# A gated attention, pooling and SSD trunk on one core: the relative position table's products moved between the turns of the first two x blocks, the branch norm done with a matrix of ones, both softmax statistics turned at once

## The chip, the core and the metric

The kernel runs on one core of one Trainium2 chip. The time is device microseconds of that core for one whole execution. Lower is better. Verdicts compare medians of several runs of the two kernels on the same chip.

## The reference, cut to what matters

One layer on x of 512 tokens by 1024 features, in float32. Three branches read the same normed input, are gated and summed, then projected; a convolutional feed-forward block follows.

```python
u = rmsnorm(x, ln1_g[i])
proj = u @ w_in[i]
q, k, v, pool_in, z, xbc, dt_raw, gate_pre = jnp.split(proj, split_idx, axis=-1)
y_a = dilated_attention_mixer(q, k, v, rel_bias) @ w_a[i]
y_b = pool_mixer(pool_in, pool_w[i], pool_scale[i]) @ w_b[i]
y_c = ssd_mixer(z, xbc, dt_raw, ...) @ w_c[i]
gates = jax.nn.sigmoid(gate_pre + b_gate[i]).reshape(b, s, N_BRANCH, D_MODEL)
merged = gates[:, :, 0] * y_a + gates[:, :, 1] * y_b + gates[:, :, 2] * y_c
x = x + merged @ w_o[i]
x = x + conv_ffn(rmsnorm(x, ln2_g[i]), ...)
out = rmsnorm(x, final_g)

# attention: three groups of six heads, dilations 1, 4, 16, each a causal band
bias = bias_table[bucket]                      # the relative position table
m = max(scores); p = exp(scores - m); l = sum(p)
o = (p @ v) / l; lse = m + log(l)
alpha = softmax(stack(lses), axis=groups)      # the groups are weighed by lse
o = sum(alpha * o)

# the SSD branch's norm, over each of two groups of 512 features
y = y.reshape(b, s, SSD_INNER) * jax.nn.silu(z)
yg = y.reshape(b, s, SSD_GROUPS, SSD_INNER // SSD_GROUPS)
yg = yg * lax.rsqrt(jnp.mean(yg * yg, axis=-1, keepdims=True) + NORM_EPS)
y = yg.reshape(b, s, SSD_INNER) * norm_w
```

## The kernel before, in words

Every large product is made of fp32r matmuls in three parts: each factor is split into a high part (a cast to fp32r on ACT) and a low part (the difference, on DVE), and high*high, high*low and low*high are summed in PSUM (`mm3`, L234). Tokens or features are laid on the 128 partitions, 512 on the free side. Weights come in blocks called jobs of 1 MB or less. For job n the kernel issues, before its products, the low part of job n+1 (L215, `wl`), the cast of job n+2 in two halves (L195, `wh`) and the fetch of job n+3 (L183, `raw`, two buffers). The fetch waits until the low part that read the buffer before is done.

The order on PE, ACT, DVE and POOL is the order in which the program issues instructions (`ORDERED`). Each of these engines runs its own list in that order and waits only for data and buffers. SP is left out of that list: a planner places its DMAs, by the times that it works out, and they need not stand in the order of the program.

Small work is threaded between the large products by coroutines. `step()` is called after each 128-feature chunk of a product (24 matmuls of 512 columns for eight k-blocks). It takes one coroutine from `waiting` into `running` and advances all of those that run by one `yield`. Within a step there are phases (0, ROWS, WHOLE, REST); `yield WHOLE` holds the coroutine until that phase of the same step, where the transposes and small products of PE stand. Thus a coroutine's instructions of one step stand on each engine's list behind those of the coroutines that joined `running` earlier, and before the next job's low part.

PSUM has eight banks: four tagged "mm" for the large products, four tagged "sm" for the small ones. SBUF tiles of 128x512 float32 come from one pool of 54 slots through `T(name)`.

The places that the change touches:

- The opening (`load_x`, `warm_up`, `turn_scale`, the loop over two blocks). x is loaded as eight tiles of 128 tokens by 512 features (`xin`). For the first two token blocks the row norm's factor is put on the diagonal of a matrix (`diag`, from the identity `eye`), and PE turns the block with it (`uT`, L1574): one product both transposes and scales. Twelve warm-up products run before that. g1 (the norm's weight) is turned between the two blocks (L1590) and copied by DVE (L1591). `turned` writes uh (ACT) and ul (DVE); `begin` (L1557) makes the first two chunks of the pool branch's projection.
- `bias_rows`: loads the bias table and a one-hot table (`hot`, 33 rows by 896) and returns `rows`, in which PE multiplies the two (`psr`, L532, four products in float32), DVE copies the result (`rv`), and SP stores it in DRAM (`rdram`) and reads it back in shifted rows as six tiles `b`. `rows` ran as a coroutine behind the pool branch's first products, inside the first group's v product (`pb`, a flipped product with 400 columns).
- `attend(g)`: attention of one group. The row maxima (`nm`) and sums (`ls`) of six heads by four blocks are turned at the end by `stats`, eight transposes into two banks (`pst`, L786), and copied by DVE (`nmT`, `lsT`). `combine` makes the groups' weights of them: on DVE up to the reciprocal (L811), POOL's product (L815), stores to DRAM (`wd`), and 18 loads `wb`, by which POOL multiplies the outputs `o` (L824).
- `ssd_prep`: per-head constants, among them `dgc`, which holds the skip weight and the norm's weight.
- `gated(gi, j, z)` and `y_norm(gi)`: y*z and its square for each of four chunks of a half (`sq`, ACT); the squares are summed by POOL and, the last, by DVE (L1094). Then `y_norm` sums over the features on PE (`pss`, L1104, four float32 products with one column), `rstd_of` makes the reciprocal square root on ACT and DVE, DVE puts it on four diagonals (`dg`, L1108), and PE spreads it over all partitions by a product with ones (`prb`, L1115). DVE multiplies y by it (L1118), and y is split into `yth` and `ytl`.

Around the branch norm the order is given by `MIX = "ZZ0zz1ggggaa"`: two z jobs of the first half, y_norm(0) queued, two z jobs of the second half, y_norm(1) queued, four jobs of the third gate, then the attention's output product.

Of the kernel before, what the change touches and what calls it, by code (L numbers as in the profile page):

```python
# [10 lines left out]
F32 = mybir.dt.float32  # L11
# [72 lines left out]
def trunk(ctx: ExitStack, tc, out, x, rel_bias, ln1_g, w_in, b_gate, w_a, pool_w, pool_scale, w_b,  # L84
# [37 lines left out]
    ones = cpool.tile([P, P], F32, name="ones")  # L122
# [388 lines left out]
    def bias_rows():  # L511
# [4 lines left out]
        sp.dma_start(relb[:BUCKETS, :18], rel_bias)  # L516
        sp.dma_start(hot[0][:BUCKETS + 1, :S], c_hot[:, :S])
        sp.dma_start(hot[1][:BUCKETS + 1, :R_ALL - S], c_hot[:, S:])
# [5 lines left out]
        def rows():  # L524
            rv = [T(f"rv{i}") for i in range(2)]
            rd = dram.tile([HEADS, R_ALL], F32, name="rdram")
            ps_r = [SM("psr0"), SM("psr1")]
            for g, (off, n) in enumerate(zip(R_OFF, R_LEN)):
                lo = off
                while lo < off + n:  # L530
# [3 lines left out]
                    lo += m  # L534
            for i in range(2):
                m = (S, R_ALL - S)[i]
                dve.tensor_copy(rv[i][:HEADS, :m], ps_r[i][:HEADS, :m])
                sp.dma_start(rd[:, i * S:i * S + m], rv[i][:HEADS, :m])
# [8 lines left out]
            return  # L547
            yield
# [23 lines left out]
    dtr = cpool.tile([P, 4, SH], F32, name="dtr")  # L572
    V, QK, OT, NM, LS = {}, {}, {}, {}, {}
# [133 lines left out]
    def attend(g):  # L707
        nm = cpool.tile([P, 4, HEADS], F32, name=f"nm{g}")
        ls = cpool.tile([P, 4, HEADS], F32, name=f"ls{g}")
# [71 lines left out]
        def stats():  # L781
            yield WHOLE
            for src, store, nme in ((nm, NM, "nmT"), (ls, LS, "lsT")):
                ps = SM("pst")
                for n in range(4):
                    pe.transpose(ps[:HEADS, n * P:(n + 1) * P], src[:, n, :], eye)  # L786
                t = T(nme)
                dve.tensor_copy(blocked(t[:HEADS], g), grouped(ps[:HEADS], g))
                store[g] = t
# [114 lines left out]
    def ssd_prep():  # L904
# [39 lines left out]
        pe.matmul(ps[:, n16:2 * n16], ones, a, start=True, stop=True)  # L944
        for i, r in enumerate((dr, gr)):
            pe.transpose(ps[:, 2 * n16 + 8 * i:2 * n16 + 8 * i + 8], r[:8, :P], eye[:8, :8])
        dve.tensor_copy(dgc, ps[:, 2 * n16:2 * n16 + 16])
        acs, tot, dec = (f(nme) for nme in ("acs", "tot", "dec"))
# [35 lines left out]
    def ssd_item(c, gi):  # L984
        cs = slice(c * P, (c + 1) * P)
        dtv, acs, dec, tot, ad, ed = (cst[n] for n in ("dtv", "acs", "dec", "tot", "ad", "ed"))
# [109 lines left out]
    def y_norm(gi):  # L1096
        while len(SQ[gi]) < 4:
            yield
        yield
        yield  # L1100
        yield WHOLE
        ps = SM("pss")
        for tb in range(4):
            pe.matmul(ps[:, tb:tb + 1], SQ[gi][0][:, tb * P:(tb + 1) * P], ones[:, :1],  # L1104
                      start=True, stop=True)
# [600 lines left out]
```

## Time and profile before

| | before |
|---|---|
| median of 3 runs | 1039.63 us (1039.3 to 1040.51) |
| the profiled execution, its own time | 1039.95 us |
| its span, first to last instruction | 1038.0 us |
| mean granted TensorE clock | 0.996 |
| instructions | 13344 |
| HBM read, written | 110.87 MB, 2.22 MB |

The profile is of one execution. The span leaves out 1.95 us that lie around the first and last instruction. Each engine's busy time is the time that its instructions take; PE's matmuls are pipelined, so the starts of two matmuls lie closer than the length of one. PEld is the load of the stationary side, which overlaps the matmul before it. A float32 product appears as two instructions, an fp32r product as one, a float32 transpose as one. The chain of waits is followed back from the last instruction to what released it; its pieces give the start, the length and what ran. A group of rows that starts with a time is the timeline: start, length, engine, line, operation, out<-in, and how often, with the idle time before it and what ended that in brackets.

### The profile page before, as it was taken

The numbers are of one execution on the slowest core, as the hardware profiler recorded it, in microseconds if no ns is written. First come the engines' busy times: TensorE is split into PE (matmuls) and PEld (weight loads), VectorE is DVE, ScalarE is ACT, GpSimd is POOL, SyncE is SP. The second block draws the span as 40 slices with busy tenths as digits, with TensorE's granted clock in tenths as the row PEclk, the third lists the DMA queues.
The fourth block names the chain that finished last, engine by engine and source line by source line (L and its number), as shares of the span: only waits on it lengthen the run. The fifth ranks groups of instructions, "written<-read, shape, count | busy, mean of one in ns | idle before, by whom it ended". The sixth has DMA issues, their size and how long they took to land.

```text
span 1038.0 us, 13344 instructions
## 1 busy us (share of the span) xinstructions
PE 1026.6 (99%) x5304; PEld 863.0 (83%) x5304; DVE 707.7 (68%) x947; ACT 488.7 (47%) x790; POOL 136.9 (13%) x118
## 2 busy tenths in 40 slices
PE   8999999999999999999999999999999999999997
PEld 8988877899888887788888888898888888888885
DVE  4563556778756649566658756767778769876776
ACT  5432445444574362566554324545445544444332
POOL 1680000000000001100143500001111100111002
PEclk9999999999999999999999999999999999999999
DMA  8445222124322354541253525443231232412222
GB/s 272 130 108 157 85 79 75 31 77 147 123 82 81 82 158 107 141 136 48 81 154 124 200 82 203 166 142 122 82 107 56 81 122 89 155 41 81 81 81 82
DMA packets 112302, 115.54 MB, mean 111 GB/s; under 512 B 5204, under 2 KB 97175, under 8 KB 112240
## 3 DMA queue, kind: packets, MB, share of 16 engines
q1 hardware_dynamic: 111647, 113.83, 35.5%
q8 instruction: 42, 0.69, 0.3%
q10 hardware_dynamic: 592, 0.86, 0.2%
q14 instruction: 21, 0.16, 0.1%
HBM read 110.87 MB, written 2.22 MB: 109 GB/s over the span
## 4 chain that ended last, share of the span: by engine, by line
PE 94%; DMA 2%; DVE 2%; ACT 1%; issue 1%; ACTq 0%; DVEq 0%; SPq 0%
PE pa L234 35%; PE pu L234 22%; PE pb L234 11%; PE pd L234 7%; PE pqk L234 6%; PE pa L1557 2%; PE pu L1363 1%; PE pq L234 1%; PE ps L731 1%; PE pt L760 1%; PE ppw L234 1%; PE po L772 1%; DMA w<-in_w_in_dram 1%; PE py L1045 1%; DMA eye<-in_c_eye_dram 1%
## 5 line engine op out<-in xcount | busy, mean ns | idle before, releaser
L215 DVE TENSOR_TENSOR wl<-raw,wh 128x2048 fp32r<-128x2048 f32 (+3 forms) x93 | 213.4, 2295 | 47.8 <-ACT wh L195 42.5
L195 ACT CAST wh<-raw 128x1024 fp32r<-128x1024 f32 (+3 forms) x184 | 183.6, 1017 | 40.1 <-DMA raw<-in_ffn_w_down_dram 12.9
L234 PE MATMUL pa<-uh,wh 128*128 128x512 f32 x384 | 99.5, 401 | 0.0
L1236 DVE SCALAR_TENSOR_TENSOR hc<-pu,fcol,hc 128x510 f32<-128x510 f32 x88 | 65.8, 748 | 49.0 <-ACT hc L1233 47.3
L234 PE MATMUL pa<-ul,wh 128*128 128x512 f32 x384 | 95.0, 389 | 0.0
L234 PE MATMUL pa<-uh,wl 128*128 128x512 f32 x384 | 94.8, 389 | 0.0
L234 PEld LDWEIGHTS pa<-ul,wh 128*128 128x128 f32 x384 | 72.1, 188 | 15.3
L234 PEld LDWEIGHTS pa<-uh,wl 128*128 128x128 f32 x384 | 72.1, 188 | 14.9
L234 PE MATMUL pu<-uh,wh 128*128 128x512 f32 (+1 forms) x352 | 83.6, 379 | 0.0
L234 PE MATMUL pu<-uh,wl 128*128 128x512 f32 (+1 forms) x352 | 83.5, 379 | 0.0
L234 PE MATMUL pu<-ul,wh 128*128 128x512 f32 (+1 forms) x352 | 83.5, 379 | 0.0
L234 PEld LDWEIGHTS pa<-uh,wh 128*128 128x128 f32 x384 | 70.2, 188 | 15.6 <-issue 1.7
L234 PEld LDWEIGHTS pu<-uh,wl 128*128 128x128 f32 x352 | 64.2, 188 | 12.4
L234 PEld LDWEIGHTS pu<-ul,wh 128*128 128x128 f32 x352 | 64.2, 188 | 12.4
L234 PEld LDWEIGHTS pu<-uh,wh 128*128 128x128 f32 x352 | 64.1, 188 | 12.4
L1241 POOL TENSOR_TENSOR hc<-hc 128x512 f32<-128x512 f32 x22 | 31.7, 1441 | 288.6 <-DVE hc L1236 253.6
L1233 ACT ACTIVATE hc<-pu,fcol,fcol 128x512 f32<-128x512 f32 x40 | 31.2, 780 | 79.1 <-PE pu L234 79.1
L1013 POOL TENSOR_TENSOR xd<-xc,dec 128x512 f32<-128x512 f32 x6 | 6.4, 1061 | 357.3 <-issue 308.8
L753 ACT ACTIVATE sb<-sb,nm 128x128 f32<-128x128 f32 (+1 forms) x72 | 30.1, 419 | 30.4 <-DVE nm L750 17.7
L1134 ACT ACTIVATE sg<-pa,col 128x512 f32<-128x512 f32 x24 | 16.5, 688 | 46.1 <-PE pa L234 46.1
L215 DVE TENSOR_TENSOR wl<-w,wh 128x2048 fp32r<-128x2048 f32 (+1 forms) x14 | 29.9, 2136 | 5.4 <-ACT wh L195 5.4
L1238 ACT ACTIVATE hc<-hc 128x512 f32<-128x512 f32 x22 | 13.9, 632 | 40.8 <-DVE hc L1236 40.8
(371 smaller groups left out, 1886.6 us busy)
## 6 DMA issues: line engine op xcount, KB each, us to landing
raw<-in_w_in_dram SPq DMA_DIRECT2D x25, 1024.0 KB, 6.3
raw<-in_ffn_w_up_dram SPq DMA_DIRECT2D x22, 1024.0 KB, 5.3
raw<-in_w_o_dram SPq DMA_DIRECT2D x8, 1024.0 KB, 5.1
raw<-in_w_in_dram SPq DMA_DIRECT2D x14, 512.0 KB, 4.1
raw<-in_ffn_w_down_dram SPq DMA_DIRECT2D x6, 1024.0 KB, 5.0
raw<-in_w_in_dram SPq DMA_DIRECT2D x6, 768.0 KB
raw<-in_w_b_dram SPq DMA_DIRECT2D x4, 1024.0 KB, 5.0
al<-ad SPq DMA_DIRECT2D x16, 256.0 KB, 7.0
```

Of the source, the lines that this page charges most:

```text
L195: act.copy(job.high[:, :, o], job.raw[:, :, o])
L215: (eng or dve).tensor_tensor(l[:, :, o], job.raw[:, :, o], h[:, :, o].bitcast(F32), OP.subtract)
L234: pe.matmul(ps, l, r, start=first and n == 0, stop=last and n == total - 1)
L731: pe.matmul(pss[i][:, o:o + w * P], q[r, n * P:(n + 1) * P], k[r, kb * P:(kb + w) * P], start=True, stop=True)
L753: act.activation(sb[:, off:off + w * P], sb[:, off:off + w * P], AF.Exp, bias=nm[:, n, h:h + 1], accum_out=ls[:, n, h:h + 1])
L760: pe.transpose(pt[:, o:o + P], sb[:, o:o + P], eye)
L1134: act.activation(s, ps, AF.Sigmoid, bias=col[:, o:o + 1])
L1233: act.activation(t, ps, AF.Identity, bias=ff["c1"][:, ff["b"] + m:ff["b"] + m + 1], scale=fw(2, m))
L1236: dve.scalar_tensor_tensor(t[:, sh:], ps[:, :S - sh], fw(k, m), t[:, sh:], OP.mult, OP.add)
L1238: act.activation(t, t, AF.Silu)
L1241: pool.tensor_tensor(a, a, t, OP.mult)
L1557: pe.matmul(first[2 * n + j][:, lo:hi], a[:, k, j * P:(j + 1) * P], b[:, k, lo:hi], start=a is wh and b is uh and k == 0, stop=a is wl and ...
```

## The change

The loads of the bias table and of the one-hot table are issued by ACT ahead of its first table load, where SP issued them later. The halves of the first two x blocks are shared between SP's queue and ACT's, and the identity is second on ACT's queue where it was third. The square sum of the second block's second half is DVE's where it was ACT's. The table's four products stand between the turns of the first two blocks, in two banks that `begin` uses later, and the copies, stores and loads behind `turned` of these blocks. In the branch norm the summed squares are split into a high part (ACT) and a low part (DVE), and two fp32r products with a matrix of ones give the sum over the features in all partitions at once; ACT makes exp(-ln/2) of it and its square, and two DVE instructions refine it (the factor -1/(2*512) is put into the norm's weight in `dgc`). `nm` and `ls` become two parts of one tile of 38 columns per block, one tile for all groups, so that `stats` makes four transposes into one bank. Two constants of `ssd_prep` reuse older tiles.

```diff
@@ -119,7 +119,8 @@
 
     eye = cpool.tile([P, P], F32, name="eye")
     tri = cpool.tile([P, P], F32, name="tri")
-    ones = cpool.tile([P, P], F32, name="ones")
+    ones = cpool.tile([P, P], F32R, name="ones")
+    eps = cpool.tile([P, 1], F32, name="eps")
 
 
     waiting, running = [], []
@@ -513,18 +514,15 @@
 
         relb, hot = T("relb"), [T(f"hot{i}") for i in range(2)]
         dve.memset(relb[:, :18], 1.0)
-        sp.dma_start(relb[:BUCKETS, :18], rel_bias)
-        sp.dma_start(hot[0][:BUCKETS + 1, :S], c_hot[:, :S])
-        sp.dma_start(hot[1][:BUCKETS + 1, :R_ALL - S], c_hot[:, S:])
+        act.dma_start(relb[:BUCKETS, :18], rel_bias)
+        act.dma_start(hot[0][:BUCKETS + 1, :S], c_hot[:, :S])
+        act.dma_start(hot[1][:BUCKETS + 1, :R_ALL - S], c_hot[:, S:])
 
         def part(tiles, lo, n):
             i = lo // S
             return tiles[i][:, lo - i * S:lo - i * S + n]
 
-        def rows():
-            rv = [T(f"rv{i}") for i in range(2)]
-            rd = dram.tile([HEADS, R_ALL], F32, name="rdram")
-            ps_r = [SM("psr0"), SM("psr1")]
+        def rows(ps_r):
             for g, (off, n) in enumerate(zip(R_OFF, R_LEN)):
                 lo = off
                 while lo < off + n:
@@ -532,6 +530,9 @@
                     pe.matmul(part(ps_r, lo, m)[:HEADS], relb[:BUCKETS + 1, 6 * g:6 * g + 6],
                               part(hot, lo, m)[:BUCKETS + 1], start=True, stop=True)
                     lo += m
+            yield
+            rv = [T(f"rv{i}") for i in range(2)]
+            rd = dram.tile([HEADS, R_ALL], F32, name="rdram")
             for i in range(2):
                 m = (S, R_ALL - S)[i]
                 dve.tensor_copy(rv[i][:HEADS, :m], ps_r[i][:HEADS, :m])
@@ -544,8 +545,6 @@
                                   ap=[[1, P], [R_ALL, 2], [1, width]])
                     sp.dma_start(b[:, at:at + 2 * width].rearrange("p (h c) -> p h c", h=2), src)
                 bias.append(b)
-            return
-            yield
 
         return rows
 
@@ -570,6 +569,8 @@
         return ap if g == 0 else ap.rearrange("p (r j) -> p r j", r=4)
 
     dtr = cpool.tile([P, 4, SH], F32, name="dtr")
+
+    both = cpool.tile([P, 4, 32 + HEADS], F32, name="nmls")
     V, QK, OT, NM, LS = {}, {}, {}, {}, {}
 
     def v_jobs(g):
@@ -705,8 +706,7 @@
                                                           lambda i, ps: emit("q", 1, i, r3[i], ps))]
 
     def attend(g):
-        nm = cpool.tile([P, 4, HEADS], F32, name=f"nm{g}")
-        ls = cpool.tile([P, 4, HEADS], F32, name=f"ls{g}")
+        nm, ls = both[:, :, :HEADS], both[:, :, 32:]
         if g == 0:
             banks = [[(1, 0, 2), (2, 1, 2)], [(3, 2, 2), (0, 0, 1)]]
         else:
@@ -780,13 +780,12 @@
 
         def stats():
             yield WHOLE
-            for src, store, nme in ((nm, NM, "nmT"), (ls, LS, "lsT")):
-                ps = SM("pst")
-                for n in range(4):
-                    pe.transpose(ps[:HEADS, n * P:(n + 1) * P], src[:, n, :], eye)
-                t = T(nme)
-                dve.tensor_copy(blocked(t[:HEADS], g), grouped(ps[:HEADS], g))
-                store[g] = t
+            ps = SM("pst")
+            for n in range(4):
+                pe.transpose(ps[:32 + HEADS, n * P:(n + 1) * P], both[:, n, :], eye)
+            for at, store, nme in ((0, NM, "nmT"), (32, LS, "lsT")):
+                t = store[g] = T(nme)
+                dve.tensor_copy(blocked(t[:HEADS], g), grouped(ps[at:at + HEADS], g))
 
         fill([item(2 * c + hh, nb, bank) for c in range(3) for nb, bank in enumerate(banks)
               for hh in range(2)] + [after(2, stats())])
@@ -941,11 +940,12 @@
         yield WHOLE
         ps = SM("pcs")
         pe.matmul(ps[:, :n16], tri, a, start=True, stop=True)
-        pe.matmul(ps[:, n16:2 * n16], ones, a, start=True, stop=True)
+        pe.matmul(ps[:, n16:2 * n16], ones.bitcast(F32), a, start=True, stop=True)
         for i, r in enumerate((dr, gr)):
             pe.transpose(ps[:, 2 * n16 + 8 * i:2 * n16 + 8 * i + 8], r[:8, :P], eye[:8, :8])
-        dve.tensor_copy(dgc, ps[:, 2 * n16:2 * n16 + 16])
-        acs, tot, dec = (f(nme) for nme in ("acs", "tot", "dec"))
+        dve.tensor_copy(dgc[:, :8], ps[:, 2 * n16:2 * n16 + 8])
+        dve.tensor_scalar(dgc[:, 8:], ps[:, 2 * n16 + 8:2 * n16 + 16], -0.5 / S, None, OP.mult)
+        acs, tot, dec = (f(nme) for nme in ("acs", "dts", "dtz"))
         dve.tensor_copy(acs, ps[:, :n16])
         dve.tensor_copy(tot, ps[:, n16:2 * n16])
         dve.tensor_tensor(dec, tot, acs, OP.subtract)
@@ -983,7 +983,7 @@
 
     def ssd_item(c, gi):
         cs = slice(c * P, (c + 1) * P)
-        dtv, acs, dec, tot, ad, ed = (cst[n] for n in ("dtv", "acs", "dec", "tot", "ad", "ed"))
+        dtv, acs, dec, tot, ad, ed = (cst[n] for n in ("dtv", "acs", "dtz", "dts", "ad", "ed"))
         als = []
         for q in range(2):
             al = T("al")
@@ -1096,26 +1096,29 @@
     def y_norm(gi):
         while len(SQ[gi]) < 4:
             yield
-        yield
+        qh, ql = T("sqh", F32R), T("sql", F32R)
+        act.copy(qh, SQ[gi][0])
+        yield
+        dve.tensor_sub(ql, SQ[gi][0], qh.bitcast(F32))
         yield
         yield WHOLE
+
         ps = SM("pss")
-        for tb in range(4):
-            pe.matmul(ps[:, tb:tb + 1], SQ[gi][0][:, tb * P:(tb + 1) * P], ones[:, :1],
-                      start=True, stop=True)
-        r = rstd_of(ps[:, :4], 4, S)
-        dg = T("dg")
-        dve.tensor_tensor(dg.rearrange("p (b t) -> p b t", b=4), eye.unsqueeze(1).to_broadcast([P, 4, P]),
-                          r.unsqueeze(2).to_broadcast([P, 4, P]), OP.mult)
-        yield
-        yield
-        yield
-        yield WHOLE
-        ps = SM("prb")
-        pe.matmul(ps, ones, dg, start=True, stop=True)
+        pe.matmul(ps, ones, qh, start=True, stop=False)
+        pe.matmul(ps, ones, ql, start=False, stop=True)
+        r, t = T("yr"), T("yt")
+        act.activation(r, ps, AF.Ln, bias=eps, scale=1.0 / S)
+        act.activation(r, r, AF.Exp, scale=-0.5)
+        act.activation(t, r, AF.Square)
+        yield
+
+        dve.scalar_tensor_tensor(t, ps, S * EPS, t, OP.add, OP.mult)
+        dve.scalar_tensor_tensor(r, t, -3.0 * S, r, OP.add, OP.mult)
+        yield
+        yield
         for j in range(4):
             y, m = Y[gi][:, j, :], 4 * gi + j
-            dve.scalar_tensor_tensor(y, y, cst["dgc"][:, 8 + m:9 + m], ps, OP.mult, OP.mult)
+            dve.scalar_tensor_tensor(y, y, cst["dgc"][:, 8 + m:9 + m], r, OP.mult, OP.mult)
             yh, yl = T("yth", F32R), T("ytl", F32R)
             act.copy(yh, y)
             YT[m] = (yh, yl)
@@ -1429,7 +1432,6 @@
 
     def program():
         yield from jobs_a(w_in, C_POOL, 8, uhk, ulk, KD, pool_evac)
-        yield Call(lambda: waiting.append(rows_of_bias()))
         yield from v_jobs(0)
         yield from qk_jobs(0)
         yield from pool_out_job()
@@ -1495,24 +1497,27 @@
 
     xin, warm = {}, small("warm", [P, 1])
 
-    def load_x(tb, eng=sp):
+    def load_x(tb, engs=(sp, sp)):
         for h in range(2):
             t = xin[tb, h] = T("xin")
-            eng.dma_start(t, x[tb * P:(tb + 1) * P, h * S:(h + 1) * S])
+            engs[h].dma_start(t, x[tb * P:(tb + 1) * P, h * S:(h + 1) * S])
 
     g8, g1 = T("g8"), cpool.tile([P, KD], F32, name="g1")
-    load_x(0)
-    load_x(1, act)
+    load_x(0, (sp, act))
     act.dma_start(eye, c_eye)
+    load_x(1, (sp, act))
     act.dma_start(g8[:KD, :P], ln1_g[0].rearrange("(k p) -> k p", p=P))
-    dve.memset(ones, 1.0)
+    bias_table = bias_rows()
+    dve.memset(ones.bitcast(F32), 1.0)
+    dve.memset(eps, EPS)
+    dve.memset(both, 0.0)
     dve.memset(warm, 1.0)
     act.activation(warm, warm, AF.Sqrt)
     first = [MM("pa") for _ in range(4)]
 
     def warm_up(n):
         for i in range(n):
-            pe.matmul(first[3][:, :P], ones, ones, start=True, stop=True)
+            pe.matmul(first[3][:, :P], ones.bitcast(F32), ones.bitcast(F32), start=True, stop=True)
 
     fetch(weights[0], 2)
     fetch(weights[1])
@@ -1525,8 +1530,6 @@
         (b_gate[0].rearrange("(c p) -> c p", p=P), 24),
         (pool_scale[0].rearrange("(c p) -> c p", p=P), 8)], "col")
     sp.dma_start(tri, c_tri)
-    rows_of_bias = bias_rows()
-
     def row_squares(tb, ss, n=1, eng=dve):
 
         for i in range(n):
@@ -1576,7 +1579,7 @@
     for tb in range(2):
         s0, s1, v, sq, r, rt = (small(n, [P, 1]) for n in ("s0", "s1", "v", "sq", "r", "rt"))
         squares(act, xin[tb, 0], s0)
-        squares((dve, act)[tb], xin[tb, 1], s1)
+        squares(dve, xin[tb, 1], s1)
         dve.tensor_scalar(v, s0, 1.0 / D, EPS, OP.mult, OP.add)
         dve.scalar_tensor_tensor(v, s1, 1.0 / D, v, OP.mult, OP.add)
         act.activation(sq, v, AF.Sqrt)
@@ -1589,12 +1592,15 @@
                 turn_scale(0, k)
     pe.transpose(first[2][:, :KD], g8[:KD, :P], eye[:KD, :KD])
     dve.tensor_copy(g1, first[2][:, :KD])
+    bias_table = bias_table((first[2], first[3]))
+    next(bias_table)
     cast(weights[0], 2)
     low(weights[0], 2, pool)
     for k in range(KD):
         turn_scale(1, k % 2 * 4 + k // 2)
     for k in range(KD):
         turned(k, 0, bank(k))
+    next(bias_table, None)
     cast(weights[1], 2)
     parts = lows(weights[1], 2)
```

## The prediction

> **What bounds the kernel now.** I read the page first, then the chain of waits in three stretches (the opening, the old place of the bias table, the z and gate stage), then the timelines of PE, DVE, ACT, POOL and SP there. The page says that PE sets the time:
>
> ```profile
> PE 1026.6 (99%) x5304; PEld 863.0 (83%) x5304; DVE 707.7 (68%) x947; ACT 488.7 (47%) x790; POOL 136.9 (13%) x118
> ...
> PE 94%; DMA 2%; DVE 2%; ACT 1%; issue 1%; ACTq 0%; DVEq 0%; SPq 0%
> ```
>
> So a PE instruction taken away is worth its pitch on the chain, as long as PE does not meet a wait by being earlier; the other engines count only where PE would wait for them. The chain in the opening (start, length, what):
>
> ```profile
> 1.66 6.33 DMA eye<-in_c_eye_dram
> ...
> 8.51 2.50 PE uT L1574 x16
> 11.00 0.20 PE pa L1590
> 11.20 3.01 PE uT L1574 x16
> 14.21 9.59 PE pa L1557 x80
> ```
>
> PE's warm-up ends at 6.54 us; it then stands until the identity has landed (7.98) and the first diag is made. From 8.51 on it never waits. The two turns have 16 equal instructions each, yet take 2.50 and 3.01 us. The windows view says why (third figure from the right: the granted clock, ahead of the DMA share and GB/s):
>
> ```profile
> 9.00:11.00 2.00, 2.00 (x15) 1.77 (x14) 0.88 (x4) 1.97 (x2) 0.99 (x1) 0.73 1.10 336
> 11.00:13.00 2.00, 2.00 (x10) 1.98 (x10) 0.27 (x2) 0.48 (x2) 2.00 (x2) 0.50 1.09 363
> ```
>
> In finer windows the clock is 0.50 from 9.9 to 13.3 us and 1.00 on both sides. The PE pieces that the change removes, from the chain:
>
> ```profile
> 65.57 1.61 PE psr L532 x8
> ...
> 508.55 0.97 PE pst L786 x8
> 509.51 16.34 PE pa L234 x72
> 525.85 0.79 PE pss L1104 x8
> 526.64 16.50 PE pa L234 x72
> 543.13 0.86 PE prb L1115 x2
> ```
>
> and the work of POOL and DVE beside the second branch norm, which PE will newly depend on:
>
> ```profile
> 542.91 1.27 POOL L1094 TENSOR_TENSOR sq<-sq 128x512 f32<-128x512 f32 x1
> ...
> 544.21 1.76 DVE L1094 TENSOR_TENSOR sq<-sq 128x512 f32<-128x512 f32 x1 [7.59 <-POOL sq L1094]
> 545.90 3.37 DVE L215 TENSOR_TENSOR wl<-raw,wh 128x2048 fp32r<-128x2048 f32 x1
> 549.20 1.39 DVE L1118 SCALAR_TENSOR_TENSOR xs<-xs,dgc,prb 128x512 f32<-128x512 f32 x2
> ```
>
> The profiled execution took 1039.95 us (span 1038.0), the median is 1039.63; I sum against 1039.95 and carry the difference over to the median.
>
> **Branch norm.** PE's price is read start to start, so that the slowed neighbour counts too. Eight regular 512-column fp32r matmuls take 1.81. From pss (525.69) past the next eight (528.45) is 2.76, so pss costs 0.95; from prb (542.97) to 545.66 is 2.69, so prb costs 0.88; the second half has the same starts apart (549.28 to 552.04, 566.56 to 569.25). Together 3.66. In their place stand four fp32r matmuls of 512 columns, the kernel's commonest form, at 16.34/72 = 0.227: 0.91. Gain 2.75.
>
> ACT gets a cast, Ln, Exp and Square, some 0.6 to 0.7 each, and table loads of 1.28 where it had two with the square root. It stands idle 2.85 and 3.88 us around 530 and 540, and four "mm" banks lie between it and PE, so: nothing, unless it is held some 10 us. DVE loses the 2.67 and 2.19 us in which it waited for the square root, the small chain and dg, and gets two scalar_tensor_tensor (0.7 each) and one subtraction (0.7): nothing, but wl at 532.64 comes some 5 us earlier, and with it the next weight fetch (SP, 534.98), whose buffer it frees. Of the new steps only ql binds PE: the product needs it. For the first half it stands on DVE ahead of the 3.33 us reciprocal (522.80) and is done near 523.5, PE asks at 525: free. For the second half it stands on DVE behind the fourth sum of squares (waiting for POOL), wl and two products y*r. POOL's third sum at 542.91 itself stands behind o*wb, which waits for wb, and wb was queued behind the 1 MB fetch at 534.98. What decides is where SP's order puts that fetch.
>
> PE gets there at 549.28 - 0.45 (stats) - 0.50 (pss) - 0.88 (prb) = 547.4. If the fetch now goes ahead of the wb loads (issued near 529.5, where wl allows it), its 3 us at the 350 GB/s seen there are over by 534, the sixth wb (issued near 534.9, at best 2.8 to land) is there at 537.7, the third o*wb done at 539.0, POOL's sum at 540.3. DVE's sum and wl took 1.76 and 3.37 beside a busy POOL and take 0.67 and 2.28 elsewhere; halfway, with two products (1.4) and ql (0.7), that is 1.2 + 2.8 + 2.1: 546.4, or 547.5 if both are slowed in full. PE would wait 0 to 0.1; I take 0.5 for what I can't see of the order. If the order stays, the fetch is some 1.5 us earlier and ql ends at 549.75: a wait of 2.35 (a rival).
>
> **Statistics.** Eight transposes cost (511.18 - 508.48) - 1.81 = 0.89 at the third group, 0.93 at the first. Four remain; their stationary side has 38 columns in place of 6 (loads of 128 columns take 138 ns, of 6 columns 86, both beside the matmul). Four full transposes (pt) cost 0.44 on the chain. Half of 0.9, three times: gain 1.35. The two DVE copies stay. The groups now share one tile, so a group's first maximum waits for the last group's transposes: these are at 192, 329 and 509, long before the next group starts. The added 0.16 us in ssd_prep and the memsets lie where DVE is not waited for.
>
> **Bias table.** At its old place PE loses 24 regular pb matmuls' rhythm from 65.43 to 67.21 (67.94 less one step of 0.73): gain 1.78. DVE's copies (1.14) and SP's two stores and nine loads leave 71.6 to 78.8, where PE does not wait. They now stand near 20 us: DVE stood 1.30 there (until 19.33, for ACT's squares), which covers 1.14 by a hair; without that cover PE would wait up to 1.1 at its turn at 23.54. On SP they pass the fetches at 19.60 and 24.10, cast only at 34.52 and 42.73: free at 6.3 us to land.
>
> The opening: ACT issues three more DMAs ahead of its table load. Their kin on SP have a pitch of 0.36, ACT's own 0.45: 1.1 to 1.45 us. So s0, at 5.26 before, comes at 6.35 to 6.7; v started at 6.40 before, held by xin's second half, which now leads ACT's queue. I take v at 6.5. From v to the end of diag took 1.21 + 0.35 without the identity's wait, so PE starts at 8.2 (8.1 to 8.5) instead of 8.51. The first turn runs at full clock nearly to its end: 16 at 0.11 (L1622's pitch), to 10.05; g1's transpose to 10.3. DVE, with the second block's square sum now its own (0.7), ends diag at 10.4 and g1's copy at 10.6; the table's products, which overwrite g1's bank, start at 10.65. At half clock until 13.33, 1.34 of their 1.61 are done, the rest at 13.6; then the second turn at full clock, 1.75: 15.35, against 14.21. Cost 1.14. The casts and evictions behind shift along.
>
> **Two rules of the Trainium skill.** The identity landed 6.33 us after its issue, behind 512 KB in ACT's queue; now 256 KB stand ahead of it, and I take it as no longer late. DMA: Bandwidth & Descriptors (Issuing engines are not separate DMA queues) says that issuing from several engines saves only the issue time; by it the identity stays near 8.0 and PE starts at 8.5, which adds 0.3 to the sum. No row here separates the two.
>
> The clock fell 1.4 us after PE resumed from 1.95 us of standing and came back 3.4 us later. TensorE: Matmul & The Clock Gate (What's actually happening) says that the gate watches a free-running window of about 3.4 us; the 3.4 us agree, and by the free run the fall may be missing in another execution, a rival below.
>
> **Sum.** +1.14 - 1.78 - 1.35 - 2.75 + 0.5 = -4.24: 1035.7 for a profiled run, 1035.4 beside the median.
>
> **Rivals.** (1) SP's order stays as it was: ql makes PE wait 2.35 in place of 0.5: -2.39, 1037.2. For it: SP's order in the trace is not the program's. Against: wl frees the buffer before the first wb can be read back. 0.22. (2) Slower: the sqh, sql, yr and yt tiles take slots from the pool of 54 that also holds the wb tiles (SP waited 0.4 us for PE at L822, a slot's release), so wb loads come late, and POOL's third sum with them. Every us counts in full once ql is late. In the old order a third sum 2.4 us later makes the change worthless; 5 us later, about what a wb load took to land (4.9), gives -2.39 + 5 = +2.6, 1042.2. 0.13. (3) The one-hot table is late: x loads took 6.5 us to land, grow 8.5; issued at 3.9, the table lands at 10.4 to 12.4. At 12.4 the products end at 14.5, the turn at 16.25: +2.04 instead of 1.14, 1036.3. 0.09. (4) The clock stays up: the products end at 12.2, the second turn at 14.0, so the opening costs -0.2: 1034.1. For it, a shorter stand; against, the fall in this trace. 0.08. Forecast: 0.48.
>
> **Numbers.** The range runs from case 4 with half a us of spare to a little past case 1: 1033.6 to 1038.9, leaving out case 2 and a tail below. About 0.2% (2.1 us) is what a measurement of this kernel can tell from no change. Faster by more: the forecast, cases 3 and 4 and half of case 1 (which lies 0.3 beyond the line), rounded down for waits I have not seen: 0.70. Same: the other half of case 1 and small misses: 0.17. Slower: case 2: 0.13.
>
> **What would show it.** After: no psr between the pb products; four transposes in each pst group; pss as two matmuls at 0.23; begin's first products near 15.35; the second y_norm's ql ending before PE's pss, or a wait "PE pss <- DVE sql" of 2 us or more (case 1 or 2). SP's fetch stands ahead of the first wb if my order holds. PE waiting on hot, or on slots, would make the sum wrong, and so would any new wait at L234 after 510 us.

## The result, and the profile after

The changed kernel takes 1048.83 us (median of 6 runs, 1046.02 to 1051.17) against 1039.49 for the kernel before: a ratio of 1.009 with a 95% interval of 1.008 to 1.010. It is slower by some 9.3 us, where 4.2 us faster was forecast. The profiled execution took 1048.91 us with a span of 1046.8, against 1039.95 and 1038.0. Runs of the kernel before lie at two levels, near 1037.7 and near 1039.5, as the clock does or does not stay up in the opening; where a part is worth less than that, the text compares executions with the same clock there.

PE has 28 instructions fewer and is busy as long as before; the line of the page on the chain says where the rest of the span is (PE had 94% of it, ACT 1%):

```profile
PE 1027.2 (98%) x5276; PEld 863.5 (82%) x5276; DVE 711.8 (68%) x944; ACT 494.7 (47%) x796; POOL 139.5 (13%) x118
...
PE 93%; DVE 2%; ACT 2%; DMA 1%; issue 1%; SPq 0%; POOL 0%; DVEq 0%; ACTq 0%; POOLq 0%
```

PE's waits (us in total, times, longest) name two places. Before, the longest of all was 1.9.

```profile
PE pss L1108 <- DVE sql L1102: 6.1, 1, 6.1
PE uT L1577 <- DVE diag L1589: 3.8, 1, 3.8
```

The same landmarks in the two chains give the account. The first long run of `begin` starts at 34.89 in place of 27.86: +7.03. Past the old place of the table, `pqk` starts at 85.81 in place of 80.57: -1.79. The three groups of statistics give -0.42, -0.46 and -0.50. Between the last of these (512.79 in place of 509.51) and the v product behind the gates (641.66 in place of 632.88) lies the branch norm: +5.50. The rest is -0.6; most of it lies between the first group's statistics and the second group's attention, where the change alters nothing.

**The opening**, in the timeline of ACT and then the chain (start, length, what):

```profile
2.90 0.32 ACTq L517 DMA_DIRECT2D relb<-in_rel_bias_dram  x1
4.39 0.31 ACTq L518 DMA_DIRECT2D hot<-in_c_hot_dram  x1
5.45 0.30 ACTq L519 DMA_DIRECT2D hot<-in_c_hot_dram  x1
5.79 1.28 ACT L1515 ACT_TABLE_LOAD   x1 [5.79 <-DMA xin<-in_x_dram]
...
7.19 0.61 ACT L437 ACTIVATE junk<-xin 128x512 f32<-128x512 f32 x1
```

```profile
1.19 4.25 DMA xin<-in_x_dram
5.43 0.02 issue
5.45 0.30 ACTq L519
...
9.59 3.78 PE uT L1577 x16
13.37 0.21 PE pa L1593
13.59 0.02 issue
13.61 0.18 DVE g L1594
13.79 0.04 issue
13.83 3.15 PE pa L530 x8
16.98 3.71 PE uT L1577 x16
20.69 10.13 PE pa L1560 x80
```

The loads are not issued one behind the other: after the first, 1.17 and 0.75 us of waiting lie ahead of the next two. The chain names what ended the second wait: an x load that landed at 5.43. The trace's list of semaphores says why. The first eight loads of SP and ACT each have a counter of their own that tells of the landing. The ninth and the eleventh, the two of the one-hot table, take the counters of the first and third load again, both x loads, and are issued only when these have landed. ACT's table load therefore stands at 5.79 in place of 2.89, the square sum at 7.19 in place of 4.53, and PE starts at 9.59 in place of 8.51. From there the pieces of the chain are longer, since the clock is down (windows of PE: busy time, granted clock, DMA share, GB/s):

```profile
7.00:9.00 2.00, 0.00 (x0) 0.79 1.15 288
9.00:11.00 2.00, 1.41 (x6) 0.50 1.11 323
...
19.00:21.00 2.00, 2.00 (x11) 0.50 1.05 382
21.00:23.00 2.00, 2.00 (x16) 0.80 1.07 386
```

In windows of half a microsecond the clock is 0.50 from 8.16 to 21.82, 13.66 us, where before it was down for 3.4.

**The second branch norm**, in the chain from SP's fetch to PE's product, and on POOL and DVE (timelines; the bracket is the idle time before):

```profile
536.65 6.37 DMA raw<-in_w_in_dram
543.02 0.02 issue
543.03 0.45 SPq L821
...
544.16 3.29 DMA wb<-wd
...
547.83 1.29 POOL sq L1094
...
550.83 3.37 DVE wl L216
554.19 3.34 DVE xs L1121 x2
557.53 0.61 DVE sql L1102
558.14 0.04 issue
558.19 0.79 PE pss L1108
```

```profile
530.17 6.09 POOL L814 TENSOR_TENSOR nmT<-nmT,dtmp 6x512 f32<-6x512 f32 x3 [19.84 <-DVE dtmp L810]
536.23 1.28 POOL L1094 TENSOR_TENSOR sq<-sq 128x512 f32<-128x512 f32 x1
544.10 3.77 POOL L823 TENSOR_TENSOR o<-o,wb 128x512 f32<-128x512 f32 x3 [6.58 <-DMA wb<-wd]
```

```profile
549.14 1.76 DVE L1094 TENSOR_TENSOR sq<-sq 128x512 f32<-128x512 f32 x1 [10.47 <-POOL sq L1094]
...
554.12 3.41 DVE L1121 SCALAR_TENSOR_TENSOR xs<-xs,dgc,yr 128x512 f32<-128x512 f32 x2
```

The order is read from the top: POOL's three products nmT take 6.09 us where they took 4.04; SP's stores wait for them, the 1 MB fetch is issued behind the last store, the wb loads behind the fetch, and one of these waits (1.2 us) until the fetch has landed at 543.02. So POOL waits 6.58 us for wb, its third sum is late, DVE waits 10.47 for that sum, and then the sum, wl, two products of y with the norm's factor (y*r, tile xs) and the low part ql (tile sql) take 9.0 us in a row before PE gets its second product.

### The profile page after: what moved, and what is told of

Its sections match the earlier page's. It is cut to its first block, busy times and chain, and to the rows that moved or that the text cites. A ratio compares the mean times of both kernels' runs of the same rounds, so it can differ in the third digit from the quotient of the medians.

```text
span 1046.8 us, 13286 instructions
## 1 busy us (share of the span) xinstructions
PE 1027.2 (98%) x5276; PEld 863.5 (82%) x5276; DVE 711.8 (68%) x944; ACT 494.7 (47%) x796; POOL 139.5 (13%) x118
## 4 chain that ended last, share of the span: by engine, by line
PE 93%; DVE 2%; ACT 2%; DMA 1%; issue 1%; SPq 0%; POOL 0%; DVEq 0%; ACTq 0%; POOLq 0%
PE pa L235 33%; PE pu L235 22%; PE pb L235 12%; PE pd L235 7%; PE pqk L235 6%; PE pa L1560 2%; PE pq L235 2%; PE pu L1366 1%; PE ps L731 1%; PE pt L760 1%; PE ppw L235 1%; PE po L772 1%; PE uT L1577 1%; DVE wl L216 1%; PE py L1045 1%
## 5 line engine op out<-in xcount | busy, mean ns | idle before, releaser
L1013 POOL TENSOR_TENSOR xd<-xc,dtz 128x512 f32<-128x512 f32 x6 | 6.4, 1061 | 354.0 <-DVE xc L1004 347.5
L753 ACT ACTIVATE sb<-sb,nmls 128x128 f32<-128x128 f32 (+1 forms) x72 | 30.1, 419 | 30.4 <-DVE nmls L750 17.7
```

What stands on the lines that cost most here:

```text
L753: act.activation(sb[:, off:off + w * P], sb[:, off:off + w * P], AF.Exp, bias=nm[:, n, h:h + 1], accum_out=ls[:, n, h:h + 1])
```

## The experiments

**The three parts, each alone.** First the opening with the table at its new place, in the kernel before:

```
kernel before + bias_rows / load_x / squares / next(bias_table) of the change
(statistics and branch norm as before)
```

> The kernel before with the opening's part of the change alone (loads on ACT's queue, x halves shared, table's products between the turns). Theory A (the opening lost 7.0 us of PE time and gave back 1.8 at the table's old place): 5.2 us slower than before, PE's first turn near 9.6 us, granted clock 0.50 from there to about 21 us. Rival (the opening's loss needs the other parts, or is a matter of one profiled run): within 2 us of before.

Measured: 1041.9 (1041.08 to 1045.35, 8 runs), ratio 1.0036 [1.0022, 1.005]. The late issue is the same (one-hot loads at 4.37 and 5.64, table load at 5.97, PE's start at 9.77), yet the long run of `begin` starts at 31.16, +3.3 and not +7.0: the clock fell only from 9.79 to 13.2, and the table's products took 1.68 in place of 3.15. Three of the eight runs lie at 1044.3 to 1045.4, 3 us above the others. So the part costs 1.5 us net with a short fall and more with a long one; the 5.2 us of the theory are met by the slower three alone.

```
kernel before + y_norm, dgc and constants of the change
```

> The kernel before with the branch norm's part alone. Theory B (the second half's low part comes late, since POOL's third sum waits behind products that wait for the wb loads, and these stand behind the 1 MB fetch in SP's order): PE waits about 6 us for sql, time +5 to +6 us (product saving 2.75, wait 6, clock fall 1, and the shift). Rival (the wait came from the other parts' shifts): no wait over 1 us, time -2 to -3 us.

Measured: 1044.31 (1043.96 to 1044.49), ratio 1.0051 [1.0034, 1.0068]. PE waits 5.4 us for sql here too, about as forecast. The branch norm alone makes the kernel slower, whatever the opening does.

```
kernel before + attend / stats of the change
```

> The kernel before with the statistics' part alone (and the two constants of ssd_prep in older tiles, without which SBUF is too small). Theory: -1.3 us, 0.42 to 0.46 for each of three groups. Rival (each gain is eaten by a later wait): 0.

Measured: 1036.08 (1035.86 to 1037.65), ratio 0.9978 [0.9968, 0.9987]. Each group of four transposes takes 0.55 in the chain where eight took 0.97. At either level of the clock it is 1.7 to 2.0 us faster than the kernel before: the full price (1.35), and a little over. Set beside the kernel before with 21 warm-up products (below; its clock stays up too), 0.4 of the 1.8 us between the two spans is the first turn, which starts at 7.91 in place of 8.31; the statistics themselves give 1.4.

**The opening.** The changed kernel with the same three loads issued by SP:

```diff
-        act.dma_start(relb[:BUCKETS, :18], rel_bias)
-        act.dma_start(hot[0][:BUCKETS + 1, :S], c_hot[:, :S])
-        act.dma_start(hot[1][:BUCKETS + 1, :R_ALL - S], c_hot[:, S:])
+        sp.dma_start(relb[:BUCKETS, :18], rel_bias)
+        sp.dma_start(hot[0][:BUCKETS + 1, :S], c_hot[:, :S])
+        sp.dma_start(hot[1][:BUCKETS + 1, :R_ALL - S], c_hot[:, S:])
```

> The changed kernel with the three loads of the tables issued by SP in place of ACT, at the same place of the program. Theory A1 (ACT's issue of the one-hot loads waits for x loads to land, and the table load and the square sum stand behind it): square sum at 4.5 us in place of 7.2, PE's first turn near 7.0 and at full clock, begin's products near 13 in place of 20.7: 6 to 8 us faster than the changed kernel, 1041 to 1043. Rival A2 (the sharing of the x halves between the queues, or the identity, makes the turn late): first turn still past 9 us, 1048.

Measured: 1043.69 (1041.88 to 1045.55), ratio 1.0046 [1.0029, 1.0063]. ACT's table load is back at 2.89, its square sum at 4.47, and PE turns the first block at 6.92:

```profile
2.89 1.28 ACT L1515 ACT_TABLE_LOAD   x1 [2.89 <-issue]
...
6.92 2.05 PE L1577 MATMUL uT<-diag,xin 128*128 128x128 f32 x16 [0.84 <-DVE diag L1589]
```

The late start thus came from ACT being held at the issue of these loads. A second wait appears behind it, in the chain:

```profile
1.66 7.13 DMA xin<-in_x_dram
8.79 0.02 issue
8.81 0.70 DVE junk L439 x2
...
11.16 2.13 PE pa L530 x8
13.29 3.71 PE uT L1577 x16
```

The second half of the second block, third on ACT's queue, lands 7.13 us after its issue; PE stands 1.84 us ahead of the table's products, and the clock falls there instead. So the long run of `begin` comes earlier by 3.3 us only, and the run is 5.1 us faster than the changed kernel, where 6 to 8 were expected.

The changed kernel with 30 warm-up products in place of 12, so that PE does not stand before the first turn:

```diff
-WARM = 12
+WARM = 30
```

> The changed kernel with 30 warm-up products in place of 12, which fill PE's stand before the first turn. Theory C (half of the opening's loss is the clock, which falls because PE stands 3.8 us): the first turn still starts at 9.6 to 9.8 us, but the clock stays at 1.00; turns 1.75 each, the table's products 1.6, begin's products from about 15.5 in place of 20.7: 5 to 6 us faster than the changed kernel, 1043. Rival (the slow products of the opening come of something else, such as the DMA traffic): no change, 1048.

Measured: 1044.37 (1043.66 to 1046.43), ratio 1.0053 [1.0034, 1.0072]. The clock is 1.00 throughout, both turns and the table's products take 1.79, 1.98 and 1.68, and the long run of `begin` starts at 30.01 where the changed kernel had 34.89. So at least 4.9 us of the opening are the fallen clock; the warm-up ends too late, at 10.51, where the changed kernel's first turn started at 9.59, and this later start hides 0.9 more.

Why the fall is long in one execution and short in another was still open. Two runs side by side: the changed kernel with the table's products behind the second block's turn, and the changed kernel again.

```diff
-    next(bias_table)
     cast(weights[0], 2)
     low(weights[0], 2, pool)
     for k in range(KD):
         turn_scale(1, k % 2 * 4 + k // 2)
+    next(bias_table)
```

> The changed kernel with the table's four products behind the second block's turn in place of ahead of it. Theory (the clock is granted in steps of about 3.41 us; a step with mostly turns brings it back, a step with a microsecond or more of the table's products, 33 rows by 6 columns, does not): PE starts at 9.6 at half clock as in the changed kernel, the clock is back at about 15, before the products, which take 1.68, and begin's products start near 18 in place of 20.69; the profiled execution is 2 to 4 us shorter than 1048.9 and the runs stay under 1047.5. Rival (the length of the fall has to do with how long PE stood, or is chance): the clock stays at 0.50 to about 21.8, begin's products start at about 20.4, and the runs spread from 1046 to 1051 as those of the changed kernel do.

> The changed kernel once more, beside the kernel with its products behind the turn, to see how its clock's fall differs between executions. Theory (steps of 3.41 us): the fall lasts a whole number of such steps, three or four, and the median is near 1048.8. Rival (the long fall of the first profile was chance): about 1045 to 1046, with a fall of one step.

Measured: 1045.57 (1045.17 to 1046.12, 5 runs), ratio 1.0066 [1.0054, 1.0078], for the first; 1047.09 (1045.28 to 1049.23, 6 runs), ratio 1.0076 [1.0062, 1.0089], for the second. The second's six runs fall into two groups, 1045.28 to 1045.98 and 1048.2 to 1049.23; the first has only the lower group. Over both measurements of the changed kernel 4 of 12 runs lie at 1046.02 or below and eight at 1048.2 or above; of the rearranged one all five lie at 1046.12 or below. The median near 1048.8 that was expected of the second was thus missed, as half of its runs are of the lower group. The rearranged kernel's profile has one short fall, 9.55 to 12.96:

```profile
9.62 3.63 PE uT L1577 x16
13.25 0.15 PE pa L1593
13.40 1.98 PE uT L1577 x16
15.38 1.60 PE pa L530 x8
16.99 9.78 PE pa L1560 x80
```

The falls of all profiles have lengths of one step or a whole number of them: 3.41 (this one), 3.41 (the opening alone), 6.8 (loads on SP), 13.66 (changed kernel) and 13.67 (again, 8.89 to 22.56), the last two being 4 x 3.415. The Trainium skill, TensorE: Matmul & The Clock Gate (What's actually happening), gives a free-running window of 3.413 us; the lengths agree. What the steps contain fits one reading: a step that PE filled with turns ended the fall, a step in which it stood for a quarter or more, or in which the table's products took about 1 us or more, did not. In the changed kernel the steps are 8.16 to 11.57 (PE standing until 9.59), to 14.99 and to 18.40 (both with the table's products, 13.83 to 16.98), and to 21.82 (turn and `begin`), after which the clock is up. The groups of the runs agree with it, but do not settle it. The rearranged kernel's one profile began its fall just as PE started, so it does not show a step that stood first, and the opening alone has one step with the products at their new place. PE stood 3.20 and 3.23 us ahead of the first turn in these two, and 3.83 and 3.68 in the two profiles with four steps, so that the length of the stand would sort them too. And three of the five rearranged runs have a mean clock of 0.991 or 0.992, below the 0.994 of the profiled one, so that it need not stand for all five. That the products of 33 rows by 6 columns count for little is the likeliest cause, and not shown.

The kernel before with 21 warm-up products:

```diff
-WARM = 12
+WARM = 21
```

> The kernel before with 21 warm-up products in place of 12, so that PE no longer stands the 1.95 us between its warm-up and the first turn of x. Theory (the clock falls because PE stands, and its fall of about 3.4 us costs some 1.6 us here): clock 1.00 from 7 to 16 us, turns of 1.8 and 1.8, begin's products from about 12.2, and about 1037.6 in every run: 1.9 under a run of before in which the clock falls, 0 under one in which it doesn't. Rival (the clock falls at a fixed time whatever PE does): clock 0.50 somewhere between 9 and 14 us as in before, 1039.5.

Measured: 1037.74 (1037.51 to 1038.12, 10 runs), ratio 0.9988 [0.9979, 0.9997]. All ten runs are at the lower level, the clock stays at 1.00, and `begin` starts at 12.48 in place of 14.21. The fall follows PE's standing; it has no fixed time. A stand of 1.82 to 1.95 us ahead of the first turn or the table's products brought a fall in five profiles, one of 1.40 (the norm with the fetch on ACT) or 1.63 (the statistics alone) none.

**The branch norm.** In each of these the kernel before has the change's branch norm. First, all sums of squares on DVE:

```diff
-            (dve if len(SQ[gi]) == 4 else pool).tensor_tensor(SQ[gi][0], SQ[gi][0], sq, OP.add)
+            dve.tensor_tensor(SQ[gi][0], SQ[gi][0], sq, OP.add)
```

> The branch norm's part alone, with all sums of squares on DVE, none on POOL. Theory B1 (sql is late because POOL's third sum stands behind products that wait for wb): the wait of PE for sql goes from 5.4 us to under 0.5; time 2 to 3 us under the kernel before, 1036.5 to 1037.5. Rival B2 (DVE itself is late, from the slower products y*r and the wait for ACT's second table load): a wait of 2 us or more stays.

Measured: 1036.33 (1035.5 to 1037.21), ratio 0.9972 [0.9962, 0.9981]. The wait at pss is gone, since the last sum now waits 0.85 us for ACT's square and not for POOL; a new wait of PE, of 0.5 us, stands later (first a line of DVE's timeline, then one of PE's waits):

```profile
536.65 0.69 DVE L1096 TENSOR_TENSOR sq<-sq 128x512 f32<-128x512 f32 x1 [0.85 <-ACT sq L1092]
```

```profile
PE pa L235 <- DVE al L836: 0.5, 1, 0.5
```

Against the kernel before at the same clock it gains 2.1 to 2.4. Second, the one 1 MB fetch issued by ACT, 3.9 us behind SP's first wb load:

```diff
-                    if n + 3 < len(weights):
-                        fetch(weights[n + 3])
+                    if job.hold:
+                        second.append(lambda: second.append(lambda: fetch(weights[n + 3], 1, act)))
+                    elif n + 3 < len(weights):
+                        fetch(weights[n + 3])
```

> The branch norm's part alone, with the one 1 MB fetch that SP issued ahead of the wb loads now issued by ACT, about 5 us later. Theory B3 (that fetch's place is what makes the wb loads late): first product with wb 3 us earlier, PE's wait for sql 5.4 down to 2 to 3 us, time 2.5 to 3.5 us under the norm's part alone (1041 to 1042). Rival B4 (wb is late from POOL's slower products nmT*dtmp, 6.2 us in place of 4.0): under 1 us gained.

Measured: 1038.22 (1035.96 to 1040.16), ratio 0.9987 [0.9977, 0.9997]. That is faster than forecast (1041 to 1042). POOL's first o*wb starts at 534.15 where it started at 538.46 in the branch norm alone, its third sum at 538.62 in place of 542.20. Of either difference 1.6 us is the opening, which was so much faster in this execution (`begin` at 25.78 in place of 27.33); 2.0 us of the sum's are left. Some 2 us more come from DVE: POOL waits for wb until 542.91, so the sum takes 0.69 in place of 1.76, wl 2.29 in place of 3.38 and two y*r 2.44 in place of 3.42, while ql takes 1.1 more. PE waits 1.3 in place of 5.4. So the fetch's place makes some 4 us of the wait, half of it because POOL no longer runs beside DVE's sum and wl. Third, PE's products one step later:

```diff
         dve.tensor_sub(ql, SQ[gi][0], qh.bitcast(F32))
         yield
+        yield
         yield WHOLE
```

> The branch norm's part alone, with PE's two products one step (one 512-column chunk, 5.4 us) later. Theory B (the products are worth their 2.75 us, only their place makes PE wait): no wait over 0.5 us, 1036.5 to 1037.5. Rival (the wait moves along, or comes again at the branch's output product, whose input is a step later): 1040 or more.

Measured: 1042.93 (1041.31 to 1043.18), ratio 1.0031 [1.0018, 1.0045]. The wait at pss is gone and another stands in its place:

```profile
PE pa L235 <- ACT ah L833: 3.6, 1, 3.6
```

ACT makes the factor later, and DVE stands at the first of its two refinements, 7.14 us in the first half and 4.14 in the second (from 565.1 to 569.27). The attention's outputs stand behind the second on DVE's list; ACT splits them (ah), and PE, which asks for ah at 569.8, gets it at 573.39. Giving PE more time only moved the wait.

**Together.** Branch norm with all sums on DVE and the statistics, with the table and the opening as before and 21 warm-up products:

```
kernel before + attend / stats, y_norm and constants of the change
              + all sums of squares on DVE, WARM = 21
```

> The branch norm and the statistics of the change, with all sums of squares on DVE, the table and the opening as before, and 21 warm-up products. If the parts add up: 1039.5 less 1.35 to 1.8 (statistics), less 2.75 (norm), less 0 to 1.9 (clock): 1033.3 to 1035.4. Rival (the norm's gain in the run with sums on DVE was partly a clock that happened not to fall, so that it counts twice): about 1035.5 to 1036.

Measured: 1034.68 (1034.59 to 1034.96, 5 runs), ratio 0.996 [0.9947, 0.9974]: 4.7 us faster than the kernel before, and 3.06 below the latter with 21 warm-up products. The gains of the two parts alone, 1.7 to 2.0 and 2.1 to 2.4, do not add in full, but the chains show why. From the third statistics to the v product behind the gates the kernel takes 121.6 us with the norm alone and in this run, and 123.4 with the old norm: 1.75 in both. The statistics give 1.4 to 1.5 in both. What each had beyond that lay elsewhere: the first turn 0.4 to 0.6 us earlier, and 0.5 us that only the profile of the kernel before spent between the opening and the statistics. The opening of this run gives 0.26 back (the long run of `begin` at 26.39 in place of 26.13). So the norm is worth 1.75 and not the 2.75 of its products; PE's wait for al, 0.6 here, is most of what I can place of the difference. DVE has little room left there: over 500 to 575 us it is busy 63.78 us in this kernel and 54.04 before.

The changed kernel with the loads on SP, 30 warm-up products and all sums on DVE:

```
changed kernel + sp.dma_start for relb and hot, WARM = 30
               + all sums of squares on DVE
```

> The changed kernel with the three table loads issued by SP, 30 warm-up products and all sums of squares on DVE. Theory (ACT's late start, the fallen clock and POOL's sums are the whole of the loss): the opening costs at most 1 to 2 us (the second block's late half still leaves PE standing up to 1.8 before the table's products), the table's old place gives 1.8, statistics and norm 4.1: 1034.5 to 1037. Rival (a fourth loss is hidden in the change): over 1039.

Measured: 1036.3 (1035.86 to 1038.24, 10 runs), ratio 0.9975 [0.9966, 0.9984]. No fourth loss of any size is hidden. It is 1.6 us behind the run above by the medians, 1.3 by the spans (1034.1 and 1032.8): `begin` starts at 15.79 in place of 12.75. Of these 3.04, 1.68 are the table's products and 1.11 the longer warm-up (first turn at 9.93 in place of 8.82). The table's old place gives 1.79 back. Moving the table's products thus buys next to nothing: they cost 1.68 in the one place and 1.78 in the other.

## Why the prediction was wrong

**Right, to the tenth.** The table's old place: 1.78 forecast, 1.79 measured. The statistics: 0.45 each forecast, 0.42 to 0.50 measured. The branch norm's price on PE: two products in place of pss and prb take 0.46 per half (pss at 522.28, the next product at 522.74, in the run of norm, statistics and warm-up together), 0.92 against the 0.91 of the sum. The order on SP, fetch ahead of the first wb load, was the one forecast. The rv copies and the nine loads of the bias rows stayed hidden.

**Wrong: the opening, +1.14 forecast, +7.03 measured.** Two steps failed.

- "Their kin on SP have a pitch of 0.36, ACT's own 0.45: 1.1 to 1.45 us." The pitch of an issue was taken as its cost. Three loads held ACT from 2.90 to 5.79, 2.9 us, because two of them waited for the landing of earlier loads. PE's start came at 9.59 in place of 8.2. With SP issuing them, ACT was back where it had been.
- "The first turn runs at full clock nearly to its end", and the clock's fall was put at 9.9 to 13.3, as before. The fall follows PE's standing, which grew from 1.95 to 3.83 us. The pieces of the chain split the +7.03: PE's start +1.08; the wait for g1's copy 0.26; the table's products at full clock 1.68; and the clock. At full clock the turns, the products and the 80 products of `begin` take 1.79, 1.98, 1.68 and 9.59 (the run with 30 warm-up products); in the changed kernel they took 3.78, 3.71, 3.15 and 10.13, 5.73 more; before, the two turns cost 1.74 more. The difference is 4.0. The sum is 7.0.

The identity's own step held: with the loads on SP it had landed by 6.51, when `diag` was made, where it had landed at 7.98 before (7.82 and 7.46 in two other profiles with the old order). The prediction had weighed a rule of the Trainium skill (DMA: Bandwidth & Descriptors, Issuing engines are not separate DMA queues), that issuing from several engines saves only the time of the issue, and had drawn from it that the identity might stay near 8.0. It did not; the rule does not speak of the place in one engine's queue, so the run says nothing against it. But the half block that took its place in the queue was late instead (7.13 us).

**Wrong: the wait for ql, 0.5 forecast, 6.1 measured.** The place was that of rival 2, with a wait of 7 or more and 1042.2, but its mechanism was not: SP waited 0.5 us for PE's slots, hardly more than before. In the time scale of before (3.28 us less at this point) the steps stand so:

- "over by 534 ... the third o*wb done at 539.0, POOL's sum at 540.3." The sum ran from 544.55 to 545.83, 5.5 us late. POOL's nmT took 2.05 us longer beside a wl that now ran at the same time; SP's fetch could not pass the stores that wait for nmT, and was issued at 533.37 and not by 531; it took 6.37 to land and not 3; and a wb load waited for its landing. With the fetch moved away the sum came 2.0 us earlier, the faster opening of that execution taken off.
- "halfway, with two products (1.4) and ql (0.7)": 6.1 us forecast from POOL's sum to ql's end, 9.0 measured. DVE's sum and wl were slowed in full (1.76 and 3.37), and two y*r took 3.41 in place of 1.39. Their third operand had come from PSUM, and now came from SBUF. The price was copied from a row with another operand.
- The price of standing was left out: the clock fell again (0.50 from 554.3 to 561.1, 6.8 us), the eight products behind pss took 3.09 in place of 1.98, and pss 0.79 in place of 0.39, some 1.5 us in all. With 6.1 and the 2.75 saved on PE this makes +4.8 of the 5.5; the rest is 0.2 of waiting for sqh and small waits that I did not place.

Rival 1's 2.35 of waiting was too small for the same reasons. Rival 3, a late one-hot table, did not come: the table's products waited 0.3 us, for g1's copy alone. Rival 4, the clock that stays up, was the wrong way about: the change made the fall longer.

## What to carry to other kernels

A DMA's price on the engine that issues it is not the pitch of an issue in a quiet stretch: count the transfers still in flight, and ask which earlier one it has to wait for. An engine on the path to the first product should issue nothing that it can leave to another. Copy a duration only from a row with the same operands, the same memories and the same neighbour, and price a new wait of PE with the clock that it loses as well as with its length.

## What the runs showed of the hardware

- DMAs of SP and ACT wait at issue for earlier ones whose counter they take: 1.17 and 0.75 us at the second and third load here, and 1.2 us of SP at a wb load until a 1 MB fetch had landed.
- DVE and POOL slow each other, but not with every operand. Two y*r with all tensors in SBUF take 1.40 beside an idle POOL and 3.41 beside a busy one; with one tensor in PSUM they took 1.39 beside a busy POOL. DVE's wl of 2048 columns takes 2.28 or 3.37, POOL's three nmT of 6x512 take 4.04 or 6.09.
- The clock falls for 3.41 us or a whole multiple of it, 13.66 at the most here. Standing for 1.82 us was enough to start a fall, standing for 1.63 was not in the one profile that has it. The kernel before loses 1.7 to 1.9 us to it in most of its executions, and nine more warm-up products take that loss away.
- Ln and Exp right behind each other loaded two tables here, 1.28 us each (ACT at 531.26 and 533.26 in the changed kernel).
